# A hybrid decoder layer: the projection's products between the mixers in steps of six passes, w_out's first part in steps of two row blocks

## The chip, the cores and the metric

The kernel runs on one core of one Trainium2 chip. The metric is the device time of one execution in microseconds, as a median of several runs. Names of the engines as the profile has them: PE is TensorE (PEld its weight loads), DVE is VectorE, ACT is ScalarE, POOL is GpSimd, SP issues most DMAs.

## The reference

One layer of a decoder over 1024 prompt tokens and 8 x 4 sample tokens (1056 in all), width 1024:

```python
h = x + 0.5 * rms_norm(swiglu(rms_norm(x, ng[0]), gate[0], up[0], down[0]), ng[1])
cols = rms_norm(h, ng[2]) @ p['w_in']
c_gla, c_gmlp, c_rwkv, c_dil = split_at(cols, [GLA_COLS, GMLP_COLS, RWKV_COLS, DIL_COLS])
# o_gla: gated linear attention in chunks of 64; o_gmlp: spatial gating in chunks of 128
# o_rwkv: RWKV-7 time mixing; o_dil: three groups of dilated windows, merged by their softmax weights
mix = jnp.concatenate([o_gla, o_gmlp, o_rwkv, o_dil], axis=-1) @ p['w_out']
h = h + rms_norm(mix, ng[3])
h = h + 0.5 * rms_norm(swiglu(rms_norm(h, ng[4]), gate[1], up[1], down[1]), ng[5])
```

Besides h, the states and the new key and value rows are returned. The sample tokens read states and caches of up to 2048 past rows from memory. All is float32.

## The kernel before, in words

A large product is made in three passes: both operands are split into a high and a low part of a reduced float32 format, and high x high, high x low and low x high are added up in PSUM (`mm3`, lines 139, 142 and 143). One call of `mm3` handles one block of 128 rows of the weight: three matmuls of 128x352, since the 1056 tokens lie in three thirds of 352.

The program has five stages: the first FFN (with a Strassen-like scheme of seven products for eight, up to about 720 us in the profile), the opening of the projection w_in, the mixers with the rest of w_in (about 800 to 1720 us), the rest of w_out with the opening of the second FFN, and the second FFN.

The change lies in the mixers' stage. The mixers are chains of small products and vector operations. Between their steps TensorE gets fill: first the products of the remaining 128-column blocks of w_in (`tile`, tiles named pw), then the first part of w_out, over the four row blocks of the gMLP and RWKV outputs (tiles pz, line 2897; the result is copied to z at line 2910). A block of w_in is 3 thirds x 8 row blocks x 3 passes = 72 passes of 128x352; w_out's first part is 4 column blocks x 9 token tiles x 4 row blocks x 3 = 432 passes of up to 128x256.

The order is made by `Loom`. It holds the fill as one generator (`line`) and the mixers' chains as others. It keeps an account of each engine's time by a cost formula of its own, and in a loop takes either a step of a chain whose operands it reckons ready, or, if there is none, one step of the fill, up to the fill's next `yield`; it takes the fill also when it reckons that TensorE's clock would fall. So a `yield` in the fill is a place at which a mixer's step may come between. On DVE (and POOL in some stages) the order so made is kept by explicit dependencies; on PE, ACT and SP the framework's own scheduling may still move instructions past each other, which is why stretches of one or two passes exist.

`products` (line 147) yields after each `mm3` but the last. `tile` (line 2812) makes one third of one block with it; with `needs`, in the opening, it waits for token tiles. In `line` the counter k of these yields sets when the next block's weights are split (`part`: ACT line 111, POOL line 112), when the one after is loaded (`load`), and when `mixes` brings in mixer outputs. In the loop of w_out's first part (line 2888 on) u counts the four row blocks; part and load hang on u == 0 and are not touched.

Of the mixers the prediction names: RWKV's chain (lines 1610 to 1755); dilated attention's scores (2065), turns (2096) and values (2107), its sample tokens' keys (2271, 2276) and values (2347, with loads cv from the cache into a ring of four), the merge (2197 to 2207); GLA's chunks (2514 to 2545), its sample tokens (2561 to 2590) and its gate (2600 to 2619). At the end the mixers' outputs are split into xl (lines 128, 129), and the rest of w_out starts (line 204).

Of the kernel before, what the change touches and what calls it, by code (L numbers as in the profile page):

```python
# [19 lines left out]
KD = 8  # L20
# [30 lines left out]
class Layer:  # L51
# [92 lines left out]
            self.pace.tick(0.45)  # L144
        return head

    def products(self, out, w, kts, m, x, cs, needs=None):

        n = len(kts)
        for i in range(n):  # L150
            if needs and not self.loom.got(needs(i)):
                yield lambda: self.loom.got(needs(i))
            self.mm3(out, w, kts[i:i + 1], m, x, cs, first=(i == 0), last=(i == n - 1))
            if i < n - 1:
                yield


# [2586 lines left out]
def third(t):  # L2744
    return slice(t * TH, (t + 1) * TH)
# [3 lines left out]
def tile_layer(ctx, tc, I, O):  # L2749
    nc = tc.nc  # L2750
    L = Layer(ctx, tc, I, O)
# [50 lines left out]
    R, W, inside = {}, {}, [0]  # L2802
# [9 lines left out]
    def tile(i, t, tag="pw", needs=None, done=None):  # L2812

        p = L.ps.tile([128, TH], F32, name="pw", tag=tag, bufs=2)
        yield from L.products(p, W[i], [(k, k) for k in range(KD)], 0, xs2, third(t), needs)
        if done:
            L.loom.after(done(p), -3)
        else:
            leave(names[i], third(t), p)

    def line():
# [25 lines left out]
        m = nn - 3  # L2847
# [20 lines left out]
        for t in range(NTH):  # L2868
            mx = mixes(K3, t - 1) if t else iter(())
            for u in range(3):  # L2870
                for k, _ in enumerate(tile(m + u, t)):
                    yield
                    if (t, u, k) == (0, 0, 0):
                        part(m + 2)
                    if (t, u, k) == (0, 1, 0):
                        load(nn)
                    if (t, u, k) == (2, 1, 0):
                        part(nn)
                    if (t, u, k) == (2, 2, 0):
                        load(nn + 1)  # L2880
                    if k == 0 or (u, k) == (1, 5):
                        next(mx, None)
                yield names[m + u] if t == NTH - 1 else None
        z = xa.tile([128, KD * T], F32, name="z", tag="xh")
# [2 lines left out]
        for q in range(4):  # L2887
            j = nn + q
            for i in ORDER:
# [3 lines left out]
                p = L.ps.tile([128, 256], F32, name="pz", tag="pw", bufs=2)  # L2893
                o, cs = p if i < 8 else p[:TS], slice(*TOK[i])
                for u, k in enumerate(K3):
# [4 lines left out]
                    if u == 0:  # L2900
# [5 lines left out]
                            part(nn + 4)  # L2906
                        if (i, q) == (7, 2):
                            load(nn + 5)
                    yield
                nc.scalar.copy(row(z, i)[:, 256 * q:256 * q + 256] if i < 8 else row(z, i)[32 * q:32 * q + 32], o)  # L2910
                yield
        yield "end"
# [62 lines left out]
    with pool("sp1") as L.sp, pool("hid1") as hp, pool("ps1", space=PSUM) as L.ps:  # L2975
# [92 lines left out]
        xs2 = L.new_xn(xa)  # L3068
# [110 lines left out]
```

## Time and profile before

| what | value |
|---|---|
| median of 3 runs | 2524.47 us (2524.19 to 2533.98) |
| the profiled execution | 2542.71 us |
| its span | 2541.0 us |
| mean granted clock of TensorE in it | 0.967 |
| PE busy | 2450.6 us, 96% |
| DVE, POOL, ACT busy | 1399.0, 1069.6, 1013.3 us |
| pw passes (lines 139, 142, 143) | 888 of each kind |
| pz passes (line 2897) | 288 and 144 |

The profile is of one execution, 18.2 us longer than the median. A matmul's length in it overlaps the next one's start, so the distance of two starts is what a pass costs; a float32 product of the mixers stands as two rows of the trace, one pass as one. The granted clock is told as a share of full speed.

### The profile page before, as it was taken

To read this page: it belongs to the slowest core of one execution; us is meant where nothing else is said; L and a number is where in the kernel's file an instruction comes from. 1 tells how busy PE (TensorE), PEld (TensorE's weight loads), DVE (VectorE), ACT (ScalarE), POOL (GpSimd) and SP (SyncE) were. 2 spreads that over 40 slices of the span, in tenths; PEclk is the share of its full clock that TensorE was granted. 3 is DMA by queue.
4 is the path that set the end of the run, shared out by engine and by line. 5 is a ranking of instruction groups with operands and counts; after the bars stand their busy time and mean duration, and the time that the engine had idled before them with its cause. 6 is when DMAs were issued, how large, how long until landed. Compare 5 with 4: busy or idle time off the path is not lost. (4 is left out here: it accounts for less than half of the span.)

```text
span 2541.0 us, 41010 instructions
## 1 busy us (share of the span) xinstructions
PE 2450.6 (96%) x15543; PEld 2242.1 (88%) x15543; DVE 1399.0 (55%) x3211; ACT 1013.3 (40%) x2175; POOL 1069.6 (42%) x902
## 2 busy tenths in 40 slices
PE   8999999999989999999999999998999999999997
PEld 7999999977789988888888888857989999997777
DVE  7645454467684156665533556337854444436767
ACT  5333333366554332233225434324533333336651
POOL 3655555577642233232111101113255555557764
PEclk9999999999999989999999889698999999999999
DMA  4322222333434333232226556254232222232334
GB/s 130 91 68 84 69 84 68 108 86 108 130 119 124 97 96 88 84 96 67 56 78 213 169 173 206 59 179 140 89 98 67 82 66 81 68 112 81 108 107 146
DMA packets 273612, 265.21 MB, mean 104 GB/s; under 512 B 36283, under 2 KB 247380, under 8 KB 273414
## 3 DMA queue, kind: packets, MB, share of 16 engines
q1 hardware_dynamic: 223810, 212.69, 28.4%
q10 hardware_dynamic: 49604, 49.90, 5.8%
q8 instruction: 122, 2.00, 0.3%
q14 instruction: 76, 0.62, 0.1%
HBM read 195.26 MB, written 67.16 MB: 103 GB/s over the span
## 5 line engine op out<-in xcount | busy, mean ns | idle before, releaser
L520 POOL TENSOR_TENSOR wlo<-wraw,whi 128x512 fp32r<-128x512 f32 x280 | 379.5, 1374 | 357.0 <-ACT whi L519 357.0
L549 PE MATMUL p<-xh,whi 128*128 128x352 f32 x1120 | 364.7, 326 | 5.5 <-DVE hid L475 3.5
L551 PE MATMUL p<-xh,wlo 128*128 128x352 f32 x1120 | 362.9, 324 | 0.0
L550 PE MATMUL p<-xl,whi 128*128 128x352 f32 x1120 | 361.9, 323 | 0.0
L519 ACT CAST whi<-wraw 128x512 fp32r<-128x512 f32 x280 | 166.6, 620 | 411.5 <-PE p L550 292.1
L139 PE MATMUL pw<-xh,whi 128*128 128x352 f32 x888 | 308.8, 348 | 4.9 <-ACT stg L2782 2.3
L112 POOL TENSOR_TENSOR wlo<-wraw,whi 128x1024 fp32r<-128x1024 f32 x61 | 146.7, 2406 | 390.8 <-ACT whi L111 354.2
L143 PE MATMUL pw<-xh,wlo 128*128 128x352 f32 x888 | 295.6, 333 | 0.0
L142 PE MATMUL pw<-xl,whi 128*128 128x352 f32 x888 | 295.1, 332 | 0.0
L549 PEld LDWEIGHTS p<-xh,whi 128*128 128x128 f32 x1120 | 211.9, 189 | 6.9 <-DVE hid L475 3.8
L550 PEld LDWEIGHTS p<-xl,whi 128*128 128x128 f32 x1120 | 212.1, 189 | 0.0
L551 PEld LDWEIGHTS p<-xh,wlo 128*128 128x128 f32 x1120 | 211.1, 189 | 0.0
L139 PEld LDWEIGHTS pw<-xh,whi 128*128 128x128 f32 x888 | 172.0, 194 | 14.1 <-issue 4.9
L142 PEld LDWEIGHTS pw<-xl,whi 128*128 128x128 f32 x888 | 172.4, 194 | 3.1 <-issue 2.3
L143 PEld LDWEIGHTS pw<-xh,wlo 128*128 128x128 f32 x888 | 171.9, 194 | 1.6 <-issue 1.3
L549 PE MATMUL p<-hid,whi 128*128 128x352 f32 x400 | 130.0, 325 | 2.2 <-ACT n L583 1.2
L551 PE MATMUL p<-hid,wlo 128*128 128x352 f32 x400 | 129.8, 324 | 0.9 <-POOL wlo L520 0.9
L550 PE MATMUL p<-hid,whi 128*128 128x352 f32 x400 | 129.1, 323 | 0.0
L723 PE MATMUL p<-xh,hid 128*128 128x512 f32 x320 | 109.7, 396 | 0.0
L204 PE MATMUL pt<-whi,ya 128*128 128x256 f32 x512 | 97.7, 290 | 1.1 <-POOL ya L793 1.1
L111 ACT CAST whi<-wraw 128x1024 fp32r<-128x1024 f32 x61 | 64.0, 1049 | 87.1 <-PE pw L142 56.2
L839 DVE TENSOR_TENSOR y<-y,p 128x512 f32<-128x512 f32 x112 | 76.7, 686 | 38.1 <-PE p L723 36.0
(642 smaller groups left out, 5939.9 us busy)
## 6 DMA issues: line engine op xcount, KB each, us to landing
wraw<-in_w_ff_gate_dram SPq DMA_DIRECT2D x44, 512.0 KB
wraw<-in_w_ff_up_dram SPq DMA_DIRECT2D x44, 512.0 KB
wraw<-in_w_in_dram SPq DMA_DIRECT2D x37, 512.0 KB
wraw<-in_w_ff_down_dram SPq DMA_DIRECT2D x36, 512.0 KB
hid_d<-tmp ACTq DMA_DIRECT2D x60, 176.0 KB
hid_d<-n ACTq DMA_DIRECT2D x60, 176.0 KB
cv<-in_cache_win_dram SPq DMA_DIRECT2D x36, 256.0 KB
whi<-hid_d SPq DMA_DIRECT2D x32, 256.0 KB
```

The lines of the kernel that those rows point to most:

```text
L112: nc.gpsimd.tensor_tensor(lo, raw, hi.bitcast(F32), op=OP.subtract)
L139: ins = nc.tensor.matmul(out, a, xh[:, cs], start=(first and i == 0), stop=False)
L142: nc.tensor.matmul(out, a, xl[:, cs], start=False, stop=False)
L143: nc.tensor.matmul(out, b, xh[:, cs], start=False, stop=(last and i == n - 1))
L204: nc.tensor.matmul(out, xs[kx][a][:, cs], ws[js[0]][b][:, kw], start=u == a == b == 0, stop=u == len(kk) - 1 and a == 1, skip_group_check= ...
L519: nc.scalar.copy(t[0][:, i], v)
L520: nc.gpsimd.tensor_tensor(t[1][:, i], v, t[0][:, i].bitcast(F32), op=OP.subtract)
L549: nc.tensor.matmul(out, ah, xh, start=first and k == 0, stop=False, skip_group_check=True)
L550: nc.tensor.matmul(out, ah, xl, start=False, stop=False, skip_group_check=True)
L551: nc.tensor.matmul(out, al, xh, start=False, stop=k == KH - 1, skip_group_check=True)
L723: nc.tensor.matmul(out, a[i][:, u], b[j][:, u], start=first and u == i == j == 0, stop=u == n - 1 and i == 1, skip_group_check=True)
L839: (nc.vector.tensor_copy if h else nc.scalar.copy)(v, p) if copy else nc.vector.tensor_add(v, v, p)
```

## The change

`products` gets a parameter `by`: it yields after each `by`-th call of `mm3`. `tile` gives 2 where nothing is waited for, that is for all fill between the mixers, so that six passes stand between two yields instead of three; the opening keeps 1. w_out's first part yields after two row blocks (six passes) instead of one. The one place where k is compared with a later value is set from 5 to 2, the same point in passes (18 done). At k == 0 and k == 1, six and twelve passes are now done, where it was three and six.

```diff
-    def products(self, out, w, kts, m, x, cs, needs=None):
+    def products(self, out, w, kts, m, x, cs, needs=None, by=1):
...
             self.mm3(out, w, kts[i:i + 1], m, x, cs, first=(i == 0), last=(i == n - 1))
-            if i < n - 1:
+            if i < n - 1 and i % by == by - 1:
                 yield
...
-        yield from L.products(p, W[i], [(k, k) for k in range(KD)], 0, xs2, third(t), needs)
+        yield from L.products(p, W[i], [(k, k) for k in range(KD)], 0, xs2, third(t), needs, 1 if needs else 2)
...
-                    if k == 0 or (u, k) == (1, 5):
+                    if k == 0 or (u, k) == (1, 2):
                         next(mx, None)
...
                             part(nn + 4)
                         if (i, q) == (7, 2):
                             load(nn + 5)
-                    yield
+                    if u % 2:
+                        yield
                 nc.scalar.copy(row(z, i)[:, 256 * q:256 * q + 256] if i < 8 else row(z, i)[32 * q:32 * q + 32], o)
```

The instructions stay the same in kind and number; their order changes from the mixers' stage on. PE in RWKV's first quarter (TT, NT and GN are its triangular matrices, X its columns; pw is the fill), before with minus and now with plus:

```order
+L139 MATMUL pw<-xh,whi 128x352
+L142 MATMUL pw<-xl,whi 128x352
+L143 MATMUL pw<-xh,wlo 128x352
+L139 MATMUL pw<-xh,whi 128x352
+L142 MATMUL pw<-xl,whi 128x352
+L143 MATMUL pw<-xh,wlo 128x352
 L1688 MATMUL pm<-ident,TT 128x128 x4
-L139 MATMUL pw<-xh,whi 128x352
-L142 MATMUL pw<-xl,whi 128x352
-L143 MATMUL pw<-xh,wlo 128x352
 L1210 MATMUL pm<-X,wa_7853 128x256 x2
```

Two steps of fill now stand ahead of L1688, and none between it and L1210.

PE in dilated attention where the sample tokens' keys begin (s, kT, qT and pT are the prompt's scores, keys, queries and weights; c1k and kt the sample's keys; pz the fill), before:

```order
L2107 MATMUL po<-Vn,pT 128x64 x3
L2096 MATMUL pm<-ident,s 128x128 x3
L2107 MATMUL po<-Vn,pT 128x64 x4
L2096 MATMUL pm<-ident,s 128x128 x4
L2107 MATMUL po<-Vn,pT 128x64 x3
L2096 MATMUL pm<-ident,s 128x128 x4
L2276 MATMUL pm<-qz,kt_15892 128x8 x2
L2107 MATMUL po<-Vn,pT 128x64 x4
```

and now:

```order
L2096 MATMUL pm<-ident,s 128x128 x4
L2107 MATMUL po<-Vn,pT 128x64 x3
L2096 MATMUL pm<-ident,s 128x128 x3
L2276 MATMUL pm<-qz,kt_15901 128x8 x4
L2276 MATMUL pm<-qz,kt_15908 128x8 x4
L2897 MATMUL pz<-whi,xl 32x256 x2
L2897 MATMUL pz<-wlo,xl 32x256
L2897 MATMUL pz<-whi,xl 32x256 x2
```

Before, no fill stood among the first L2276; now 22 passes follow them. By the first L2276, 192 pz passes stood ahead before, and 290 now.

PE at the end of the mixers (cv and A or Z: values and weights of the sample tokens; gq, gk, gaT, gSF, gex, gkn: GLA's sample tokens; on: the merge), before:

```order
L2347 MATMUL pm<-cv,Z 16x256
L2206 MATMUL pm<-ident,on 128x128 x2
L2897 MATMUL pz<-whi,xl 128x256
L2897 MATMUL pz<-wlo,xl 128x256
L2897 MATMUL pz<-whi,xl 128x256 x2
L2347 MATMUL pm<-cv,Z 16x256 x3
L2897 MATMUL pz<-wlo,xl 128x256
L2897 MATMUL pz<-whi,xl 128x256 x2
```

and now, down to the first product of the next stage:

```order
L2576 MATMUL pgo<-gq,gSF 128x4 x8
L2347 MATMUL pm<-cv,Z 16x256 x8
L2358 MATMUL pm<-ident,A 128x128 x3
L2206 MATMUL pm<-ident,on 128x128 x2
L2606 MATMUL pm<-gb2m,gaT 32x2 x2
L2589 MATMUL pm<-gex,gkn 32x512 x4
L2206 MATMUL pm<-ident,on 128x128 x2
L2616 MATMUL pm<-ident,gsp 128x32 x2
L2206 MATMUL pm<-ident,on 128x128 x2
L204 MATMUL pt<-whi,xl 128x256
```

Before, fill lay among L2347 to its last; now the last pass stands before the 40th of its 72, and GLA's sample products, which stood among the fill, stand behind it. In both orders 2664 pw passes and 432 pz passes stand between the same ends.

## The prediction

> **What bounds the kernel now.** I read the page first, then the table by stretches of time, then the fill instructions alone, then the timeline of single places. The page:
>
> ```profile
> span 2541.0 us, 41010 instructions
> PE 2450.6 (96%) x15543; PEld 2242.1 (88%) x15543; DVE 1399.0 (55%) x3211; ACT 1013.3 (40%) x2175; POOL 1069.6 (42%) x902
> PEclk9999999999999989999999889698999999999999
> ```
>
> TensorE bounds it: no other engine passes 55%. But the digits of the granted clock fall in slices 26 to 30, so inside the mixers TensorE is busy and slow at once. The three mixer stages by time (RWKV; dilated attention with GLA while columns of the projection are left; then w_out's first part as fill), and one piece of the first FFN:
>
> ```profile
> 800.00:1334.00 534.00, 516.02 (x3679) 469.26 (x3678) 261.44 (x820) 154.65 (x344) 135.26 (x137) 0.98 0.30 84
> 1334.00:1546.00 212.00, 205.32 (x1300) 181.88 (x1300) 103.98 (x378) 90.48 (x269) 27.60 (x29) 0.89 0.61 183
> 1546.00:1720.00 174.00, 166.76 (x1113) 129.81 (x1113) 72.73 (x232) 60.33 (x167) 27.44 (x24) 0.86 0.47 142
> 160.00:200.00 40.00, 40.00 (x250) 39.86 (x250) 18.69 (x22) 13.78 (x28) 23.16 (x18) 1.00 0.25 81
> ```
>
> Columns: stretch, length, busy time and count of PE, PEld, DVE, ACT, POOL, clock, DMA share, GB/s. TensorE's idle time is 18 + 7 + 7 us in 920 us; what the clock takes is 534 x 0.02 + 212 x 0.11 + 174 x 0.14 = 58 us. So the order of work matters through three things: how often TensorE changes between fill and small products, whether fill lies where the clock would fall, and what is left at the end without fill. I call one matmul of fill a pass.
>
> **Changing over: what a merged visit saves.** First a visit of the small products in RWKV, then two in the dilated sample phase (start, length, matmuls):
>
> ```profile
> 1135.55 0.32 PE L139 MATMUL pw<-xh,whi 128*128 128x352 f32 x1
> 1135.73 1.16 PE L1712 MATMUL pm<-work,NT 128*128 128x128 f32 x8
> 1136.64 0.40 PE L142 MATMUL pw<-xl,whi 128*128 128x352 f32 x1
> 1136.88 0.32 PE L143 MATMUL pw<-xh,wlo 128*128 128x352 f32 x1
> 1137.04 0.32 PE L139 MATMUL pw<-xh,whi 128*128 128x352 f32 x1
> ```
> ```profile
> 1669.16 0.28 PE L2897 MATMUL pz<-wlo,xl 128*128 128x256 f32 x1
> 1669.28 0.27 PE L2897 MATMUL pz<-whi,xl 128*128 128x256 f32 x1
> 1669.48 0.60 PE L2347 MATMUL pm<-cv,Z 128*16 128x256 f32 x2
> 1670.02 0.39 PE L2897 MATMUL pz<-whi,xl 128*128 128x256 f32 x1
> 1671.05 1.04 PE L2347 MATMUL pm<-cv,Z 128*16 128x256 f32 x6
> 1672.01 0.39 PE L2897 MATMUL pz<-wlo,xl 128*128 128x256 f32 x1
> ```
>
> A pw pass starts 0.16 us after the one before (1136.88 to 1137.04). Into the visit it is 0.18, out of it 0.24 for the first pass: 0.02 + 0.08 = 0.10 us of changing. A pz pass takes 0.12 (1669.16 to 1669.28). Two L2347 take 0.54, six take 0.96: 0.105 each and 0.33 fixed; with 0.20 in place of 0.12 on the way in, a visit costs 0.41 us. In the orders of before and after, unbroken stretches of pw fill fall from 231 to 205 and of pz fill from 73 to 46. 26 x 0.10 = 2.6 us. Of the 27 pz visits about half lie among L2347 and half among 128-column products: 27 x (0.41 + 0.10) / 2 = 6.9. Sum **-9 us**; bounds 53 x 0.10 = 5 and 2.6 + 27 x 0.41 = 14, both gains, since the removed changes lie on the busy engine. No wait is added, but a small product that becomes ready within a step now waits up to three passes longer, 0.48 us; its chain is later by that while TensorE works, which counts only where no fill is left, at the end below. [...]
>
> **The clock: where the fill moves to.** Five stretches; the first four are cold, the last is not:
>
> ```profile
> 927.00:941.00 14.00, 11.43 (x53) 9.44 (x52) 5.41 (x16) 3.41 (x9) 1.08 (x1) 0.51 0.36 101
> 1440.00:1450.00 10.00, 10.00 (x39) 7.76 (x38) 6.16 (x26) 2.89 (x9) 0.00 (x0) 0.54 0.59 183
> 1503.00:1521.00 18.00, 18.00 (x76) 15.13 (x74) 6.83 (x20) 3.67 (x13) 1.81 (x4) 0.53 0.39 109
> 1606.00:1640.00 34.00, 33.80 (x175) 32.17 (x175) 6.33 (x22) 9.09 (x27) 2.79 (x3) 0.50 0.16 48
> 1677.00:1712.00 35.00, 35.00 (x223) 20.21 (x221) 12.56 (x50) 9.28 (x24) 4.32 (x4) 1.00 0.61 189
> ```
>
> The fourth is the plainest: 33.80 of 34 us busy, at half clock, with DVE, ACT and POOL nearly idle. What it runs is small:
>
> ```profile
> 1615.83 2.67 PE L2276 MATMUL pm<-qz,kt 128*128 128x8 f32 x12
> ```
>
> The fifth has fill between its small products and keeps the full clock. The pz passes of L2897 alone, over a stretch that holds the fourth piece and over the one behind it:
>
> ```profile
> 1546.00:1650.00 104.00, 39.30 (x220) 32.00 (x220) 0.77 0.43 128
> 1650.00:1720.00 70.00, 34.46 (x212) 26.73 (x212) 0.99 0.52 163
> ```
>
> So 212/70 = 3.0 passes per us go with a clock of 0.99, 220/104 = 2.1 with 0.77. The new order uses the fill sooner in terms of the small products. Counted between the same small products, the four cold stretches get 33, 23, 38 and 64 more passes. Lost in them now: 14 x 0.49 + 10 x 0.46 + 18 x 0.47 + 34 x 0.50 = 37 us. If all became warm, 37 us would come back; if none, nothing. I take 14: the fourth gets its passes in clumps before 1626 and almost none from there to 1640, and the profiled execution is 18 us above the median, so some of its cold pieces may not be in the others. Against that, several pieces between 1378 and 1435 and between 1548 and 1601 have about 100 passes fewer; if 10 us of them fell to half clock, that would cost 5 (bounds 0 and 10). Together **-9 us**, between -37 and +10.
>
> **The end of the mixers, without fill.** At L2347's 40th instruction of 72 (each is two rows of the trace; 1677 us) before still has 112 pz passes to run; the new order has none, and GLA's sample products (L2561 to L2616) now stand behind that point too. The moved passes are paid earlier, 112 x 0.117 = 13.1 us (the spacing is 0.12 above); the stretch must shrink by as much for the move to be free. It lasts now from 1677.4 to the first L204:
>
> ```profile
> 1660.75 6.82 SPq L79 DMA_DIRECT2D cv<-in_cache_win_dram  x5
> 1654.71 3.60 SPq L79 DMA_DIRECT2D cv<-in_cache_win_dram  x4
> 1695.25 0.15 DVE L2607 TENSOR_SCALAR gst<-pm 32x4 f32<-32x4 f32 x1
> 1698.65 0.28 DVE L2610 COPY gsp<-rsy 32x256 f32<-32x256 f32 x1
> 1680.89 0.69 DVE L2590 TENSOR_TENSOR gVn<-gVn,pm 32x512 f32<-32x512 f32 x1
> 1668.31 0.58 PE L2589 MATMUL pm<-gex,gkn 32*32 32x512 f32 x1
> 1711.64 0.19 PEld L2897 LDWEIGHTS pz<-wlo,xl 128*128 128x128 f32 x1 [0.42 <-issue]
> 1718.23 0.96 DVE L129 TENSOR_TENSOR xl<-dmix,xl 128x352 fp32r<-128x352 f32 x2
> 1718.46 0.41 PE L2206 MATMUL pm<-ident,on 128*128 128x128 f32 x2 [1.24 <-DVE on L2202]
> 1718.62 0.36 PE L204 MATMUL pt<-whi,xl 128*128 128x256 f32 x1
> ```
>
> That is 41.2 us. Without fill, two chains set it. The value loads cv come two products to a load: 33 products, 17 loads. Five loads in 6.82 us are 1.36 each, so 23 us; the fastest piece (4 in 3.60) gives 15. Then the close: L2606 now comes after the last L2347, behind it four L2589 with an L2590 of 0.69 behind each 0.58 (5 us), the chain from L2607 to the end of L2610 (3.7), L2616 and L2618 (1, estimated from products and DVE operations above), four L129 (2): 12 us. 23 + 12 = 35, so the stretch shrinks by 6, not 13: **+7 us**. Bounds: 15 + 7 (today's from the end of L2347 at 1711.64 to 1718.62) = 22, which is -6; and today's loads, 4 in the 6.05 us from 1654.71 to 1660.75 or 1.5 each, with a close of 20, is 46: +18. Behind the first L204 the same products follow in nearly the same order, at nothing.
>
> The weights' split of a column moves too:
>
> ```profile
> L111 ACT CAST whi<-wraw 128x1024 fp32r<-128x1024 f32 x61 | 64.0, 1049 | 87.1 <-PE pw L142 56.2
> L112 POOL TENSOR_TENSOR wlo<-wraw,whi 128x1024 fp32r<-128x1024 f32 x61 | 146.7, 2406 | 390.8 <-ACT whi L111 354.2
> ```
>
> It is issued after six passes of the column ahead rather than three, 0.5 us later, and its 1.05 + 2.41 us lie beside the 66 passes (10 us) that are left of that column: nothing; without that cover a column would wait up to 3.5 us.
>
> Sum: -9 - 9 + 7 = **-11 us** on the profiled 2541.0 us span (2542.71 us executed). Carried to the median of 2524.47 us: **2513.5 us**.
>
> **Rivals.** First, *the clock doesn't come back*. [...] As a mechanism of this kernel: cold pieces stay cold because the extra passes come in clumps with small products for several us between them. Then -9 + 5 + 7 = +3: 2527.5 us.
>
> Second, *GLA's sample chain ends last and makes it slower*. Today it runs among fill:
>
> ```profile
> 1625.33 0.31 PE L2561 MATMUL pm<-gq,gk 32*32 32x32 f32 x2
> 1702.37 0.32 POOL L2619 TENSOR_TENSOR go<-go,ggt 128x64 f32<-128x64 f32 x1 [11.39 <-DVE mden L2176]
> ```
>
> 77 us from first to last. Most of it is waiting in TensorE's queue behind fill and L2347, which speaks against it; but now it starts after the fill is spent. If 40 us of it remain after some 15 us of L2347, the stretch takes 55 + 3: 17 us more than today and 30 more than would be free, so -9 - 5 + 30 = +16 with half the clock term's gain kept: 2540 us. It is slower than before from a stretch of about 46 us on.
>
> Third, *more comes back*: 24 of the 37 us, no new cold windows, the end 3 us dear: -9 - 24 + 3 = -30: 2494 us. For it: 158 more passes in the cold pieces. Against: the clumps.
>
> That the change doesn't do what it says is settled by the order for the most part: stretches of up to five pw passes fall from 97 to 50, not to nothing, since TensorE's final order is made afterwards.
>
> **How the numbers follow.** Forecast 0.48 (own range 2500 to 2527), clock doesn't come back 0.22, GLA's chain 0.14, more comes back 0.16. A change under about 0.5%, 12.6 us, can't be told from none. The forecast lies just inside that: 0.22 of its chance is beyond (faster), 0.26 within. With 0.16 of the third, faster is 0.38; with 0.20 of the first and 0.02 of the second, the same is 0.48; slower is 0.12 + 0.02 = 0.14. The range of 2496 to 2538 us leaves out half of the third and most of the second.
>
> **What would show it.** Right: the stretch that runs L2276 above a clock of 0.70; fewer "issue" waits before L2897; the stretch from L2347's 40th to the first L204 at 30 to 38 us, with L2897 absent. Wrong: a clock of 0.50 still beside L2276; TensorE waiting more than 5 us in all for L2616's or L2606's inputs; new cold pieces between 1378 and 1600 that take back more than 10 us.

## The result: 2498.9 us, and the profile after

| | before | after |
|---|---|---|
| median | 2524.68 us (2524.19 to 2533.98) | 2498.92 us (2493.66 to 2508.90, 4 runs) |
| ratio | | 0.990, 95% interval 0.987 to 0.993 |
| the profiled execution | 2542.71 us | 2503.86 us |
| its span, mean clock | 2541.0 us, 0.967 | 2502.1 us, 0.972 |

The change makes the kernel 1.0% faster, 26 us in the medians and 39 us in the two profiled executions. The forecast was 2513.5 us with a range of 2496 to 2538: the time lies inside it, but 1 us outside the 2500 to 2527 that the forecast named as its own, and nearer to the third rival (2494) than to the forecast. A change of this size is beyond the 12.6 us from which I called it faster, an outcome to which I gave 0.38. The page after, its first lines:

```profile
span 2502.1 us, 41009 instructions
PE 2411.0 (96%) x15543; PEld 2207.7 (88%) x15543; DVE 1395.5 (56%) x3211; ACT 1013.6 (41%) x2175; POOL 1067.8 (43%) x902
PEclk9999999999999999999989889969999999999999
```

TensorE still bounds it, with 40 us less busy time for the same 15543 matmuls. The digits of the clock have moved: slice 26, at 6 before, is full, and slice 27 is at 6 instead.

The mixers are cut best at four events: the first product of the stage (L1113), the last of RWKV's normalisation (L1293), the 40th L2347 of 72, and the first L204 behind the mixers. The stretches between them by the table of windows (length, busy time and count of PE, PEld, DVE, ACT, POOL, clock, DMA share, GB/s), before:

```profile
822.00:1317.00 495.00, 478.36 (x3443) 432.67 (x3442) 258.04 (x796) 146.54 (x329) 126.82 (x130) 0.98 0.29 82
1317.00:1685.00 368.00, 356.93 (x2324) 307.69 (x2323) 163.54 (x573) 141.16 (x407) 51.15 (x50) 0.87 0.55 163
1685.00:1719.00 34.00, 30.45 (x196) 18.83 (x193) 15.57 (x60) 12.39 (x34) 6.22 (x7) 1.00 0.49 150
```

and after:

```profile
819.00:1320.00 501.00, 490.07 (x3528) 446.12 (x3529) 257.30 (x797) 150.69 (x335) 129.48 (x131) 0.98 0.29 83
1320.00:1635.00 315.00, 307.75 (x2281) 268.05 (x2279) 162.60 (x566) 142.98 (x413) 46.75 (x47) 0.93 0.61 186
1635.00:1681.00 46.00, 29.87 (x139) 13.67 (x140) 19.38 (x70) 7.03 (x21) 5.96 (x9) 0.62 0.37 110
```

RWKV takes 6 us longer but holds 85 matmuls more, which is fill that is not left for later: at 0.16 us a pass it is 8 us to the good. Dilated attention up to the 40th L2347 is 53 us shorter. The tail is 12 us longer though it holds 57 matmuls fewer. Ahead of 822 us the two programs are the same, yet the execution after is 4 us ahead there: that much of the 39 is not the change.

**Where TensorE's time went.** I took all matmuls from the first L1113 to one common event behind the mixers (the 881st L549, at 1846 us before and 1807 after; the same matmuls but for three passes). The distance from each start to the next is what a matmul costs. Its own price is the lower quartile of that distance for its line and shape at full clock, pooled over the kernels; what is over is put down to half clock if the matmul starts in a cold piece, to a wait if it is over 0.25 us (whether or not TensorE was idle then), and else to its place: between fill and a small product, fill to fill, or among small products. This is worked out from the trace, not a view of it, and it is rough: a second working by the same rule, with shapes grouped a little differently, moved a column by up to 14 us and a difference by up to 4.

| us | length | own price | half clock | waits | fill and small | fill to fill | among small |
|---|---|---|---|---|---|---|---|
| before | 1024.0 | 741.6 | 79.0 | 68.4 | 16.1 | 27.8 | 91.0 |
| after | 988.9 | 742.5 | 72.3 | 54.4 | 9.9 | 24.0 | 85.8 |
| difference | -35.1 | +0.9 | -6.7 | -14.0 | -6.2 | -3.8 | -5.2 |

Two columns need care. Waits hold distances in which TensorE was not idle. The last product of L2347 before a pass of fill takes 0.53 us from start to start where the one ahead of it takes 0.22 (the visit at 1671.05 us in the prediction's rows). That is 0.30 us over the price, at full clock 28 times before (8.5 us) and 8 times after (2.4 us), so some 6 of the 14 us are changing over. And half clock is sorted first, so that a wait inside a cold piece counts as half clock. The idle time of TensorE over the same stretch did not fall. It was 45.9 us before:

```profile
822.50:1846.50 1024.00, 978.10 (x6758) 867.64 (x6758) 538.58 (x1750) 367.48 (x935) 226.19 (x213) 0.93 0.40 118
```

and 48.1 us after:

```profile
818.55:1807.50 988.95, 940.82 (x6755) 835.78 (x6755) 539.04 (x1750) 368.18 (x935) 224.06 (x213) 0.94 0.40 122
```

The idle time moved. By the three stretches above it went from 16.6 to 10.9 us in RWKV and from 11.1 to 7.3 up to the 40th L2347, and from 3.6 to 16.1 in the tail. In RWKV the waits are plain. What TensorE waited for between 800 and 1334 us, with the total, the times and the longest, before:

```profile
PE pm L1688 <- DVE TT L1681: 9.1, 5, 2.6
PE pw L139 <- ACT stg L2782: 2.3, 2, 1.4
```

and after:

```profile
PE pm L1688 <- DVE TT L1681: 3.8, 4, 1.2
PE pw L139 <- ACT stg L2782: 1.5, 2, 0.9
```

Six passes last 0.96 us, three 0.48, at the 0.16 from one pass to the next in both traces. L1688 stands behind them in TensorE's order and needs TT from VectorE; with six passes ahead of it, TT has come or nearly so.

This repeats. Six of the kernels profiled for this document have the order of before up to RWKV's end, and five have that of sixes. L1688 waits for 9.0 to 9.8 us in the six and for 3.8 in each of the five; TensorE is idle for 16.6 to 17.6 us of RWKV against 10.6 to 11.8. RWKV lasts 493 to 495 us in the six and 494 to 501 in the five, which do 84 passes more, 13.4 us at 0.16 each. So 7 to 14 us are gained there, 11 in the mean. That compares one order of each step only: the kernel with sixes in block 14 alone (below) gains 10 us there as well.

**The clock in the mixers.** The first run of L2276, the piece around it, the long one at full clock and the longest cold piece of all, after:

```profile
1575.90 1.85 PE L2276 MATMUL pm<-qz,kt 128*128 128x8 f32 x16
```
```profile
1575.00:1590.00 15.00, 14.98 (x162) 13.88 (x161) 5.39 (x19) 3.51 (x9) 0.19 (x1) 1.00 0.35 107
1509.00:1635.00 126.00, 122.37 (x1081) 101.31 (x1079) 72.05 (x233) 57.28 (x170) 18.28 (x20) 1.00 0.53 162
1649.00:1686.50 37.50, 23.72 (x97) 13.02 (x98) 17.87 (x52) 6.95 (x20) 7.57 (x8) 0.50 0.25 70
```

The piece at half clock that held L2276 is gone, and 126 us in a row are at full clock. A new one of 37.5 us has come in the tail, where the fill is spent. TensorE is busy for 23.7 us of it at a clock of 0.50, so by an estimate from these two numbers half clock can have cost 12 us there at most; the other 13.8 are idle.

**The weight loads of pz**, from the page's groups with the idle time ahead of them, before:

```profile
L2897 PEld LDWEIGHTS pz<-whi,xl 128*128 128x128 f32 (+1 forms) x288 | 47.8, 193 | 15.2 <-issue 11.2 <-ACT stg L2786 2.4 <-ACT z L2910 0.8
L2897 PEld LDWEIGHTS pz<-wlo,xl 128*128 128x128 f32 (+1 forms) x144 | 27.6, 191 | 4.5 <-issue 4.0
```

and after:

```profile
L2897 PEld LDWEIGHTS pz<-whi,xl 128*128 128x128 f32 (+1 forms) x288 | 44.7, 180 | 3.2 <-issue 2.1
L2897 PEld LDWEIGHTS pz<-wlo,xl 128*128 128x128 f32 (+1 forms) x144 | 26.0, 181 | 3.4 <-issue 3.0
```

**The tail.** What TensorE waited for between 1635 and 1681 us after the change:

```profile
PE pm L2206 <- DVE rst L1017: 4.1, 1, 4.1
PE pm L2589 <- DVE gex L2583: 3.2, 1, 3.2
PE pm L2347 <- DMA cv<-in_cache_win_dram: 2.5, 5, 0.7
PE pm L2616 <- DVE gsp L2610: 2.5, 1, 2.5
PE pm L2606 <- ACT dmix L2207: 1.3, 1, 1.3
```

These five are 13.6 us. Before, between 1677 and 1719 us, one line is all:

```profile
PE pm L2206 <- DVE on L2202: 3.5, 2, 2.3
```

### The profile page after: what moved, and what is told of

Same layout as the page of the kernel before. It is cut to its first block, busy times and chain, and to the rows that moved or that the text cites. A ratio compares the mean times of both kernels' runs of the same rounds, so it can differ in the third digit from the quotient of the medians.

```text
span 2502.1 us, 41009 instructions
## 1 busy us (share of the span) xinstructions
PE 2411.0 (96%) x15543; PEld 2207.7 (88%) x15543; DVE 1395.5 (56%) x3211; ACT 1013.6 (41%) x2175; POOL 1067.8 (43%) x902
## 3 DMA queue, kind: packets, MB, share of 16 engines
q1 hardware_dynamic: 223810, 212.69, 28.9%
## 5 line engine op out<-in xcount | busy, mean ns | idle before, releaser
L549 PE MATMUL p<-xh,whi 128*128 128x352 f32 x1120 | 364.0, 325 | 5.4 <-DVE hid L475 3.6
L139 PE MATMUL pw<-xh,whi 128*128 128x352 f32 x888 | 308.1, 347 | 2.3 <-ACT stg L2782 1.5
L549 PEld LDWEIGHTS p<-xh,whi 128*128 128x128 f32 x1120 | 211.4, 189 | 6.8 <-DVE hid L475 3.9
L139 PEld LDWEIGHTS pw<-xh,whi 128*128 128x128 f32 x888 | 171.5, 193 | 13.3 <-issue 7.5
L549 PE MATMUL p<-hid,whi 128*128 128x352 f32 x400 | 129.9, 325 | 1.8 <-ACT n L583 1.4
L204 PE MATMUL pt<-whi,ya 128*128 128x256 f32 x512 | 97.7, 290 | 1.0 <-POOL ya L793 1.0
```

What stands on the lines that cost most here:

```text
L139: ins = nc.tensor.matmul(out, a, xh[:, cs], start=(first and i == 0), stop=False)
L204: nc.tensor.matmul(out, xs[kx][a][:, cs], ws[js[0]][b][:, kw], start=u == a == b == 0, stop=u == len(kk) - 1 and a == 1, skip_group_check= ...
L549: nc.tensor.matmul(out, ah, xh, start=first and k == 0, stop=False, skip_group_check=True)
```

## The experiments

Each kernel was timed beside the kernel before, in four series; the median of before was 2525.8, 2526.7, 2527.4 and 2528.3 us in them, and ratios are against the same series.

### One part alone: pw in sixes

The changed kernel, but w_out's first part in steps of one row block again:

```diff
-                    if u % 2:
-                        yield
+                    yield
```

> Only the projection's products go in steps of six passes; w_out's first part keeps steps of three. Theory (the clock): what the change gains comes from fill standing where dilated attention's small products ran cold, between about 1500 and 1650 us; in this order the first L2276 has about as much fill around it as in the changed kernel, so the cold piece beside it goes and the gain is 12 to 20 of the change's 26 us. Rival (changing over): 26 fewer visits at 0.10 us, 3 us faster than before. Rival (GLA moved out): GLA's sample products stand later here too, so it agrees with the clock.

Measured: 2492.89 us (2489.53 to 2498.46), ratio 0.987 (0.984 to 0.991). All of the gain comes with pw; the intervals of this kernel and the changed one overlap (0.987 to 0.993), so that it is better is not shown. The theory of the clock had 12 to 20 of the 26 us, that of changing over 3: both were too low. It has the same RWKV as the changed kernel, and the order of what follows differs: GLA's sample products begin earlier, and from the 40th L2347 to the first L204 it takes 23 us, not 45:

```profile
1321.00:1656.00 335.00, 327.53 (x2338) 283.65 (x2338) 162.90 (x582) 144.05 (x420) 51.20 (x50) 0.90 0.58 177
1656.00:1679.00 23.00, 15.03 (x89) 4.83 (x85) 15.50 (x53) 4.77 (x15) 5.55 (x6) 1.00 0.67 195
```

The two stretches together are 358 us here and 361 in the changed kernel. What the one gains in the tail it gives up ahead of it.

### The other part alone: pz in steps of two row blocks

The kernel before, but:

```diff
-                    yield
+                    if u % 2:
+                        yield
```

> Only w_out's first part goes in steps of six passes. Here GLA's sample products stay among the first L2347 and pz fill lasts to the last L2347, as before; the L2276 piece has fill. Theory (the clock): clock over 0.8 in the stretch from the first L2271 to the first L2347, 10 to 18 us faster than before. Rival (changing over): about 7 us faster, with the cold piece still there. Rival (GLA moved out of the stretch): no gain, since GLA stays in it.

Measured: 2526.64 us (2515.40 to 2531.38, 10 runs), ratio 1.000 (0.998 to 1.002). No gain. The theory of the clock (10 to 18 us) and that of changing over (7 us) both missed; no gain is what the rival of GLA's place gave. In the order only 7 of the 27 pz visits go with this edit alone (73 stretches to 66), and 14 more with pw in sixes (60 to 46). I had priced the 27 at 6.9 us, so 7 of them at 1.8, which an interval of 0.2% to either side, 5 us, can't show. Up to 1542 us TensorE's order is that of before. The dilated part, up to the 40th L2347:

```profile
1313.00:1673.00 360.00, 341.13 (x2335) 291.24 (x2333) 168.74 (x576) 141.70 (x410) 54.90 (x51) 0.92 0.56 168
```

The clock is 0.92, where the profile of before has 0.87 up to the same product. The timed runs are closer: their mean clock is 0.974 here and 0.972 before, while the profiled execution of before, 18 us above its median, had 0.967 and was a dear one in this.

### Passes for the clock's sake alone

The kernel before, with spare 128x256 passes whose result nobody reads, four ahead of the scores of a late unit of dilated attention and two ahead of each of its turns. Loom's account leaves them out, so that the order of all else should stay (the helper `spare` and the account's part of the edit are left out here):

```diff
+        spare(Q[0], 4 if g == 0 else 0)
...
+            spare(q, 2 if g == 0 else 0)
```

> The kernel before, with 64 spare passes of 128x256 (8 in each of the last eight units of dilated attention, ahead of the scores and of the turns; nobody reads them, and the order-maker does not see them, so the order of the rest stays close to the one before). Added work at the spacing of a pass: 64 x 0.117 = 7.5 us. Theory (the clock): the cold piece of 34 us at half clock (17 us lost) becomes warm, so added work makes it faster, 3 to 10 us. Rivals (changing over; GLA moved out): 7 us slower, as work is added and nothing else changes.

Measured: 2531.72 us (2520.85 to 2540.80), ratio 1.002 (1.000 to 1.005). The trace has 50 spare passes between 1537 and 1624 us, not the 64 expected, and from the first of them on TensorE's order is not quite that of before (66 stretches of pz, not 73).

```profile
1315.00:1671.00 356.00, 344.65 (x2361) 294.80 (x2361) 161.78 (x573) 139.74 (x406) 51.54 (x50) 0.92 0.55 167
```

The clock is 0.92 in this execution, against 0.87 in that of before; but over the timed runs the mean clock is 0.972 with the spare passes and 0.972 without. So these passes did not warm TensorE enough to pay for their own 5.8 us (50 x 0.117); the median is 6 us dearer, near the 7 that the rivals of the clock expected.

### The tail kept busy

The changed kernel, with steps of six spare passes, whose result nobody reads, from the end of the fill until the mixers are done:

```diff
-        yield lambda: L.mixed == 3
+        while L.mixed < 3:
+            p = L.ps.tile([128, 256], F32, name="pj", tag="pw", bufs=2)
+            for _ in range(6):
+                nc.tensor.matmul(p, w[:, 0, 0:128], w[:, 0, 0:256], start=True, stop=True)
+            yield
```

> The changed kernel, and when the fill is spent the order-maker goes on giving TensorE spare passes of 128x256 in steps of six wherever no chain has work, to the end of the mixers (about 300; nobody reads them). The changed kernel's last stretch, from L2347's 40th instruction to the first L204, takes 46 us and is at half clock for 37 of it. Theory (the clock): the stretch gets 5 to 12 us shorter and the kernel as much faster than the changed one (2487 to 2494 us). Rival (chains of loads and of GLA's sample set the end, whatever the clock): within 3 us of the changed kernel. If the spare passes stand in the way of the chains: up to 10 us slower than the changed one.

Measured: 2510.83 us (2504.03 to 2515.27), ratio 0.994 (0.992 to 0.996), some 10 us over the changed kernel. The tail, from the 40th L2347 to the first L204:

```profile
1631.00:1685.00 54.00, 52.87 (x359) 37.92 (x359) 23.24 (x73) 8.09 (x24) 8.71 (x9) 0.97 0.32 95
```

At a clock of 0.97 instead of 0.62 the tail is 54 us, not 46. The expectation had named this: spare passes that stand in the way. The 240 of them are 28 us of work at 0.117 each, and they cost more than the higher clock gives (0.982 over the timed runs against 0.976). So what the warm clock alone would bring to the tail is not separated here. That VectorE sets the end is argued from the waits above: 11.1 of the 13.6 us are for VectorE and ScalarE.

### GLA earlier, in the changed kernel

The changed kernel with another priority for GLA's chains:

```diff
-GP = 0.9
+GP = -0.1
```

> The changed kernel with GLA's chains ahead of dilated attention's in the choice of the next small product (priority -0.1 in place of 0.9), nothing else. In its order 162 of GLA's small products stand ahead of the 71st value product (L2107) of dilated attention, as in the kernel before (154), and not 114 as in the changed one; pw and pz fill is as far along as in the changed kernel. Theory 'more fill per visit in RWKV' (87 passes are done by RWKV's end that were done later before, in time that TensorE waited): keeps the gain, 2495 to 2505 us. Theory 'GLA's products moved out of the first part of dilated attention': loses most of it, 2512 to 2525. Theory 'the clock': no statement, 2500 to 2525.

Measured: 2506.89 us (2501.27 to 2508.79), ratio 0.992 (0.989 to 0.994). It keeps most of the gain with GLA where it was before. The time lies between what the two theories gave, 2495 to 2505 and 2512 to 2525 us.

### GLA later, in the kernel before

The kernel before with the opposite:

```diff
-GP = 0.9
+GP = 2.0
```

> The kernel before with steps of three as they were and only GLA's priority lowered (2.0 in place of 0.9): 114 of GLA's small products ahead of the 71st L2107, as in the changed kernel, and the fill as far along as before at RWKV's end. 'GLA moved out': gains by itself, 2505 to 2515 us. 'More fill per visit in RWKV': no gain, 2520 to 2532, dearer if GLA's sample tokens end last.

Measured: 2509.31 us (2499.88 to 2516.01), ratio 0.993 (0.991 to 0.996): 17 us faster than before with steps of three everywhere. Taken with the one ahead, which lost 4 us of the gain by the ratios and 8 by the medians, this spoke for GLA's place as a second cause. The controls below turn it round.

### Sixes in RWKV alone, and behind RWKV alone

The kernel with pw in sixes alone, but with sixes while L.mixed is 0, which is RWKV (the other kernel: while it is 2, behind RWKV). In the first the later value of k is 5 again, the same 18 passes done; that line is left out here:

```diff
-        yield from L.products(p, W[i], [(k, k) for k in range(KD)], 0, xs2, third(t), needs, 1 if needs else 2)
+        yield from L.products(p, W[i], [(k, k) for k in range(KD)], 0, xs2, third(t), needs, 2 if L.mixed == 0 and not needs else 1)
```

> Steps of six pw passes only while RWKV runs; three again behind it, and three in w_out's first part. The order up to RWKV's end is that of the changed kernel (2202 pw passes done there against 2115 before). 'More fill per visit in RWKV': carries the gain, 2497 to 2510 us. 'GLA moved out' (134 of its products ahead of the 71st L2107, half of the way): 2510 to 2518. 'Steps of six matter in dilated attention, where the small products wait most': under a third of the gain, 2516 to 2526.

> The other half: three passes a step while RWKV runs, six behind it for the rest of the pw fill, three in w_out's first part. 2115 passes at RWKV's end as before, 162 of GLA's products ahead of the 71st L2107. 'More fill per visit in RWKV': no gain, 2518 to 2530 us. 'GLA moved out': none either. 'Six in dilated attention': 2500 to 2512. By changes between fill and small products alone (291 stretches of fill against 304 before and 265 in the kernel with pw in sixes only, which was 33 us faster): a third, 2512 to 2518.

Measured: 2502.39 us (2498.40 to 2506.66), ratio 0.990 (0.987 to 0.994), with sixes in RWKV alone; 2505.58 us (2499.11 to 2510.89), ratio 0.991 (0.988 to 0.994), with sixes behind it alone. Each half has about two thirds of the gain of both, and the two do not add up: 24 + 22 is more than 33. The first is what the theory of RWKV expected, the second what the theory of dilated attention expected, and by the expectations each excludes the other. It asks whether any other order than that of before is better.

### Nine passes a step

The kernel with pw in sixes alone, but:

```diff
-        yield from L.products(p, W[i], [(k, k) for k in range(KD)], 0, xs2, third(t), needs, 1 if needs else 2)
+        yield from L.products(p, W[i], [(k, k) for k in range(KD)], 0, xs2, third(t), needs, 1 if needs else 3)
-                    if k == 0 or (u, k) == (1, 2):
+                    if k == 0 or (u, k) == (1, 1):
```

> A further step the same way: nine passes between two stops of the pw fill (18 done at the same point as before), w_out's first part in threes. In its order 2328 pw passes are done at RWKV's end (2115 before, 2202 in the changed kernel), 242 stretches of fill against 304 before and 265 with sixes in pw alone; but the last pz pass stands ahead of the sample tokens' first value product (L2347), so some 15 to 20 us of their work more have no fill. 'More fill per visit in RWKV' and 'fewer changes': gain once more up to RWKV's end, some 10 to 20 us over the kernel with sixes, and lose as much in the tail: 2485 to 2505 us. 'The order of before is a poor draw, and any other is better': 2500 to 2515, whatever the step.

Measured: 2525.00 us (2514.51 to 2529.92), ratio 0.999 (0.996 to 1.002): the gain is gone, and neither theory of the expectation had that. RWKV gains again: with 213 passes more than before, 34 us at 0.16, it takes 512 us, so 16 us are gained there against 7 to 14 with sixes. What follows takes it back. The fill pz alone, over two stretches, and all of the second:

```profile
1200.00:1630.00 430.00, 70.62 (x432) 58.16 (x432) 12.61 (x36) 0.95 0.48 142
1630.00:1713.00 83.00, 0.00 (x0) 0.00 (x0) 0.33 (x1) 0.76 0.47 142
```
```profile
1630.00:1713.00 83.00, 57.23 (x297) 25.86 (x296) 36.02 (x116) 16.25 (x41) 14.67 (x16) 0.76 0.47 142
```
```profile
PE pm L2206 <- DVE on L2202: 11.3, 2, 8.0
PE pm L2347 <- DMA cv<-in_cache_win_dram: 4.6, 5, 1.4
```

83 us go without fill (columns of the first fence: PE, PEld, ACT), TensorE is idle for 26 of them and its clock is 0.76 over them. The fill can be spent too soon: a pass moved ahead is missing here.

### Controls: another order that is no better by any count

The kernel before with sixes in one of the column blocks alone, that of index 14 (in a second kernel that of index 20); the new parameter of `products` is as in the change and left out here:

```diff
-        yield from L.products(p, W[i], [(k, k) for k in range(KD)], 0, xs2, third(t), needs)
+        yield from L.products(p, W[i], [(k, k) for k in range(KD)], 0, xs2, third(t), needs, 2 if i == 14 else 1)
```

> The kernel before with steps of six in one single column block out of the pw fill (the one with index 14, while RWKV runs); all else in threes. The order is another from there on, but by the counts it is no better: 305 stretches of fill (304 before), 2064 pw passes done at RWKV's end (2115 before), GLA's products where they were (154 ahead of the 71st L2107). 'More fill per visit' and 'fewer changes': no gain, or dearer by the 51 passes that are left, 2522 to 2535 us. 'GLA moved out': none. 'The order of before is a poor draw, and any other is better': 2500 to 2515.

> The kernel before with steps of six in one other column block (index 20), all else in threes. The order is that of before up to the last tenth of RWKV, and 2115 passes are done at RWKV's end as before; behind it it differs. By the counts it is no better: 315 stretches of fill (304 before), so 11 changes more, and 150 of GLA's products ahead of the 71st L2107 (154 before). 'The order of before is a poor draw in dilated attention, and others are better by about 10 to 25 us': 2500 to 2516 us. 'Only what the sixes save counts' (changes, and passes moved into RWKV): 2524 to 2530.

And GLA earlier in the kernel before (GP = -0.1), the opposite of what had gained 17 us:

> The kernel before with GLA's chains ahead of dilated attention's (priority -0.1 in place of 0.9): 215 of GLA's products ahead of the 71st L2107 against 154 before, 305 stretches of fill against 304; nothing else is changed, up to RWKV's end the order is that of before. 'GLA moved out' (GLA's later place gained 17 us in the kernel before): now the other way, 2530 to 2545 us. 'Fewer changes' and 'more fill per visit in RWKV': no gain, 2520 to 2530. 'The order of before is a poor draw, and any other is better': 2500 to 2515.

Measured: block 14 alone 2502.49 us (2499.82 to 2511.47), ratio 0.991 (0.987 to 0.995); block 20 alone 2521.41 us (2517.51 to 2532.58, 12 runs), ratio 0.999 (0.997 to 1.000); GLA earlier 2512.63 us (2504.58 to 2527.60), ratio 0.995 (0.992 to 0.998).

So GLA's place does not explain the gain: in the kernel before both directions gain. And a change of one block's steps can bring 23 to 25 us with no fewer changes between fill and small products and 51 passes fewer done by RWKV's end, while the same change in another block brings at most 8. Block 14 and GLA earlier are what the theory of the poor draw expected (2500 to 2515 us); block 20 fits neither that nor its rival (2524 to 2530). Block 14's kernel does in RWKV with one wait for L1688 what before did with five:

```profile
PE pm L1158 <- DVE spread L1154: 3.3, 3, 1.5
PE pm L1688 <- DVE TT L1681: 3.2, 1, 3.2
```

and holds a clock of 0.94 in the dilated part and 1.00 from the 40th L2347 to the last L2206:

```profile
823.00:1299.00 476.00, 464.84 (x3380) 420.73 (x3379) 245.49 (x791) 145.19 (x327) 124.64 (x129) 0.99 0.29 83
1299.00:1659.00 360.00, 350.07 (x2448) 298.80 (x2447) 179.24 (x616) 147.12 (x422) 57.58 (x55) 0.94 0.57 171
1659.00:1677.00 18.00, 17.75 (x113) 9.70 (x109) 6.45 (x24) 5.50 (x14) 1.74 (x3) 1.00 0.73 225
```

Block 20's kernel has 0.90 in the dilated part, about the 0.92 of the kernel with pz alone in steps of two:

```profile
1314.00:1664.00 350.00, 336.49 (x2311) 290.65 (x2312) 162.63 (x569) 140.87 (x406) 50.02 (x50) 0.90 0.55 171
```

### All of them side by side

The same account as above, by one profiled execution each; the ratio is from the timed runs. "Threes" are orders with pw in threes in all blocks but one at most, "sixes" those with pw in sixes throughout.

| us | ratio | length | half clock | waits | fill and small | fill to fill | among small |
|---|---|---|---|---|---|---|---|
| before | 1 | 1024.0 | 79.0 | 68.4 | 16.1 | 27.8 | 91.0 |
| pz in twos alone | 1.000 | 1014.4 | 60.1 | 77.5 | 15.4 | 27.2 | 92.1 |
| block 20 alone | 0.999 | 1011.1 | 63.1 | 73.2 | 16.2 | 28.9 | 87.9 |
| GLA earlier | 0.995 | 999.7 | 55.0 | 68.1 | 15.9 | 27.9 | 90.9 |
| GLA later | 0.993 | 995.1 | 56.3 | 64.3 | 14.9 | 27.3 | 90.3 |
| block 14 alone | 0.991 | 982.0 | 37.6 | 61.6 | 16.2 | 27.9 | 97.0 |
| **mean of threes** | 0.996 | 1004.4 | 58.5 | 68.9 | 15.8 | 27.8 | 91.5 |
| after | 0.990 | 988.9 | 72.3 | 54.4 | 9.9 | 24.0 | 85.8 |
| pw in sixes alone | 0.987 | 983.4 | 59.5 | 61.7 | 10.1 | 23.7 | 86.6 |
| after, GLA earlier | 0.992 | 984.7 | 40.1 | 70.5 | 14.2 | 24.5 | 95.2 |
| **mean of sixes** | 0.990 | 985.7 | 57.3 | 62.2 | 11.4 | 24.1 | 89.2 |
| sixes in RWKV | 0.990 | 992.1 | 53.4 | 70.4 | 13.7 | 24.9 | 87.9 |
| sixes behind RWKV | 0.991 | 992.0 | 43.6 | 73.0 | 15.5 | 27.2 | 90.3 |
| nines | 0.999 | 1011.4 | 69.4 | 74.2 | 11.1 | 22.9 | 91.3 |

The timed runs allow a check without the account, since each has its mean clock. Over the 69 runs of before in the four series the time falls by 2.05 us per 0.001 of clock (correlation -0.93, and 1.8 to 2.2 us in the series one by one). By that line the changed kernel's 26 us are 7 from a higher clock (0.976 against 0.972) and 19 at equal clock. It is 11 and 22 for pw in sixes alone, 12 and 12 for sixes in RWKV, 10 and 11 for sixes behind it, 11 and 11 for block 14, 10 and 7 for GLA later, 1 and 11 for GLA earlier, and under 4 in each for pz in twos, block 20 and nines. Most of what the change gains is not the clock.

Two columns follow the step: between fill and small products, and fill to fill. They fall from 43.6 to 35.5 us in the means, 8 us. Half clock and waits do not follow it: within the threes half clock goes from 38 to 79 us and waits from 62 to 78, which is more than the means differ (1 and 7 us). By the ratios, sixes are 0.0066 better than threes in the mean, 17 us; by the lengths 19. The six threes scatter by 0.004, 9 us, in the standard deviation, so three against six is a hint at 17 and not a measurement of it. The remaining 9 or so of the change's 26 us would then be that the order of before was a poor draw: none of the five other threes is slower, and three are faster beyond their intervals.

## Why the prediction was right or wrong

**Faster, and inside the range: right, in part by luck.** The sum was -11 us; the medians differ by 26, the profiled executions by 39, of which 35 lie in the mixers and 4 in the unchanged part ahead. The errors of the terms had opposite signs: the end was 18 us dearer than I had it, and gains that I had too small or not at all outweighed it.

**Changing over, -9: the right way, too small.** The two columns give -10.0 us from before to after, of which 3.8 are fill to fill, which I did not list. The changes between L2347 and pz come on top, since the account has them under waits: 0.30 us on the last product of a visit, 28 visits at full clock before and 8 after, some 6 us. I had 5.5 for half of 27 visits at 0.41; 20 went. The other visits cost 0.05 us each (16.1 us over 306 stretches of fill before, 9.9 over 251 after), not the 0.10 that I read from one.

**"No wait is added, but a small product that becomes ready within a step now waits up to three passes longer": the step that failed.** I saw only what a longer step does to a product that is ready early, and priced that at nothing where fill is left. The other side is a product that is not ready: then TensorE waits, and a longer step can cover that. My sum had no term for it, and RWKV shows it: 9.1 us for L1688 became 3.8, the idle time 16.6 became 10.9, and 85 further passes took 6 us instead of 13.6. The other kernels with these two orders of RWKV repeat it. My table of windows had the 18 us of idle time in 800 to 1334; I read it as little. Over all the mixers no idle time was saved, since the tail gave it back.

**The clock, -9: near the balance, but the place and the means are not shown.** The balance in the account is -6.7 us, and by the clocks of the timed runs 7 us. In the dilated part the clock rose more than I took, from 0.87 to 0.93 up to the 40th L2347: half clock in the account fell from 56 to 27 us there (with the waits inside the cold pieces), L2276 runs at 1.00 (above the 0.70 that I had named), and nothing is cold from 1509 to 1635. But a cold piece came in the tail, which I had not counted as a cold place; the account has 26 us of half clock there, of which the clock itself can be 12 at most and the rest is waits. That it is fill which buys the clock is not borne out: spare passes left the mean clock at 0.972. Of the 37 us that I wanted back, some belonged to that one execution: it had 0.967, where the 69 timed runs have 0.972 in the mean, about 10 us by the slope above. I named this and then discounted too little for it. I also misread the page: the digits under 9 in the mixers stand in slices 15, 23, 24, 26 and 28, not 26 to 30; the sum used the table of windows and is not touched by it.

**The end without fill, +7: wrong, it was +25, beyond my bound of +18.** Two errors. I put the 40th L2347 at 1677.4 us; the trace has it at 1684.7, since 1677.4 is the 33rd. So the stretch was 33.9 us, not 41.2, and my own 35 us would have been +14. And it took 45.3 us: 11.4 longer, where it had to shrink by 13.1 to be free. Cut at the end of the last L2347:

```profile
1635.40:1661.20 25.80, 22.68 (x115) 10.86 (x115) 6.86 (x28) 3.17 (x9) 3.16 (x4) 0.70 0.59 180
1661.20:1680.70 19.50, 6.90 (x24) 2.51 (x24) 12.49 (x43) 3.86 (x12) 2.49 (x4) 0.50 0.07 18
```

The first piece is 25.8 us, near the 23 that I gave to the loads of cv, but TensorE is busy for 22.7 of it and waited for cv for 2.5, so the loads are not what fills it. The close, to which I gave 12, takes 19.5; from 1664.7 (L2606) to 1680.7 (L204) it is 16 us with 11 us of waits in it:

```profile
1657.60 3.60 PE L2347 MATMUL pm<-cv,Z 128*16 128x256 f32 x16
1664.70 0.37 PE L2606 MATMUL pm<-gb2m,gaT 128*32 128x2 f32 x4 [1.33 <-ACT dmix L2207]
1670.11 1.92 PE L2589 MATMUL pm<-gex,gkn 32*32 32x512 f32 x4 [3.19 <-DVE gex L2583]
1676.09 0.69 PE L2206 MATMUL pm<-ident,on 128*128 128x128 f32 x2 [4.07 <-DVE rst L1017]
1679.27 0.39 PE L2616 MATMUL pm<-ident,gsp 32*128 32x32 f32 x2 [2.49 <-DVE gsp L2610]
1680.69 0.56 PE L204 MATMUL pt<-whi,xl 128*128 128x256 f32 x1
```

**The weights' split, nothing: right.** L139 waited in all for 2.3 us, and its releasers are the copies stg of its own output tiles, not the split:

```profile
L139 PE MATMUL pw<-xh,whi 128*128 128x352 f32 x888 | 308.1, 347 | 2.3 <-ACT stg L2782 1.5 <-ACT stg L2786 0.5 <-DVE stg L2780 0.3
```

**The rivals.** *The clock doesn't come back* fell as I worded it (2527.5): the clock came back in the dilated part, and most of the gain did not hang on it (7 of 26 us by the timed runs). *GLA's sample chain ends last* came about in part: it does end last, the stretch was 45 us against the 46 from which I had it slower, and TensorE waited 7.0 us for the inputs of L2616, L2606 and L2589 and 4.1 before the merge's L2206; but what was saved ahead of it was larger than the 9 + 5 us that I had set against it: the stretch up to the 40th L2347 alone is 53 us shorter. *More comes back* (2494, 0.16) is the nearest in time, and only by chance: it had 24 us from the clock, which gave 7, and an end that is 3 us dear, which was 25.

**What I named as signs.** L2276 above 0.70: 1.00. Fewer "issue" waits before L2897: 15.2 us became 5.1 in the two groups. The end at 30 to 38 us: missed, 45. TensorE waiting more than 5 us for L2616's or L2606's inputs, a sign against me: 3.8. New cold pieces between 1378 and 1600 that take back over 10 us: no, 41 us lie at half clock there after, 51 before.

**What stays open.** Which waits an order has, and where the clock falls, is not told by its counts (stretches of fill, passes done by a point, GLA's place): two kernels that differ in one block's step are 0.8% apart. Why that of block 14 is so much better than that of block 20 I cannot say from these runs. That all of the gain comes with pw in sixes is shown, and that RWKV gains 7 to 14 us between these two orders. That sixes as such, and not these orders, are better than threes by more than the 8 us of the two columns is likely and not shown.

## What to carry to other kernels

A longer step of fill covered the latency of the small products behind it here: in RWKV TensorE waited 3.8 us for L1688 where it had waited 9.1, and its idle time went from some 17 us to 11. So look at what the engine waits for, even where its idle share is 3%, price a longer step from both sides, and look also where the idle time goes: here the tail took all of it back. Fill that is moved ahead is missing at the end; at nine passes a step that took back the whole gain, so know how long the last stretch takes without any. And where the order is made by a planner, a change of steps is also a new draw of the order: time one or two neutral changes beside it (another block, another priority) before a gain under 1% is put down to the reason for which it was made.

## What was not expected of the hardware

A busy TensorE does not always have its full clock in these traces. In the five stretches below, of the two profiled executions, TensorE is busy throughout or nearly so. The columns are those of the products of all matmuls in the stretch, added up:

| stretch, us | length | PE busy | clock | matmuls | columns | columns per us |
|---|---|---|---|---|---|---|
| before, 160 to 200 | 40.0 | 40.00 | 1.00 | 250 | 88000 | 2200 |
| before, 1677 to 1712 | 35.0 | 35.00 | 1.00 | 223 | 55240 | 1578 |
| after, 1575 to 1590 | 15.0 | 14.98 | 1.00 | 162 | 17280 | 1152 |
| after, 1389.6 to 1406.7 | 17.1 | 17.10 | 0.50 | 70 | 12928 | 756 |
| before, 1606 to 1640 | 34.0 | 33.80 | 0.50 | 175 | 13504 | 397 |

The last is the fourth stretch of the prediction; 126 of its 175 matmuls have 8, 64 or 128 columns. The two at half clock have the fewest columns per us. But a pw pass behind another starts 0.29 us after it at half clock and 0.16 at full clock (medians, before and after alike), so a stretch at half clock has fewer for that reason too, and cause and effect are not separated. What brings the clock down these runs do not show. The pieces at half clock last 3.4, 6.8, 13.7, 17.1, 20.5 or 37.5 us after the change, but for the one at the kernel's end.

One kernel's executions differ by more than I had allowed for: those of before lie between 2510 and 2546 us over the four series, and most of that goes with the clock that they had (correlation -0.93). The half clock in the mixers of orders that share most of their products' sequence lies between 60 and 79 us.
